# A flow-matching step on one core, its instruction order made with the builder's other machine model

## The chip, the cores and the metric

The kernel runs on one core of a Trainium2 chip. The metric is the device time of one execution in microseconds, as the median of several; less is better. All engines of the core work in parallel on streams of their own: PE (matmuls, and PEld for its weight loads), DVE (VectorE), ACT (ScalarE), POOL (GpSimd) and SP (SyncE, which here issues loads). Each engine takes its instructions strictly in the order of its stream and waits, by semaphores, for what an instruction needs from other engines.

## The reference

One inference step of a two-layer backbone of width 1024, with 512 latent tokens (a grid of 8 rows by 64 columns), 128 prompt tokens and 256 cached prompt keys. Layer 0 mixes tokens by attention with 16 heads: a latent query sees a window of the grid, with a learned bias, and the cached keys, in one softmax; prompt tokens attend among themselves. Layer 1 mixes them by a bidirectional linear recurrent unit (LRU). Each mixer and each feed-forward network (FFN) is wrapped the same way:

```
def _modulate(x, g, shift, scale):
    return _rms_norm(x, g) * (1 + scale[:, None, :]) + shift[:, None, :]
...
def _swiglu(x, w_gu, w_down):
    gate, up = jnp.split(x @ w_gu, 2, axis=-1)
    return (jax.nn.silu(gate) * up) @ w_down
```

The shift, scale and gate vectors come from a conditioning vector times a large matrix (the modulation, six vectors per layer). Each sublayer's output times its gate is added to x. A last RMS norm ends the step, and new keys, values and final LRU states are returned.

## The kernel before, in words

Activations lie transposed, features on the 128 partitions in eight blocks, the 640 tokens along the free dimension. Every product of two float32 matrices is made of three: both operands are split into a high part (a cast by ACT: weights at L180, activations at L1325 and others) and a low part (raw minus high, by DVE: L182 for weights, L1327 for activations), and PE computes high by high (L227), high by low (L228) and low by high (L229), accumulated in PSUM. A weight comes in 512 KB pieces by SP's queue into `raw`, of which there are three, as there are of `whi` and `wlo`. The products go to `mm` tiles (three PSUM buffers), each half of the tokens (320 columns) 24 matmuls long.

The stages, with the times of the profiled execution: start, with norm and first projections (0 to 55 us); attention (55 to 322); its output projection (322 to 370); FFN of layer 0 (370 to 830); LRU (845 to 1005); the LRU's output projection (1005 to 1070); FFN of layer 1 (1070 to 1500); the end.

*Attention.* `attend` goes through eight pairs of heads. A pair is four blocks of 128 queries for each of two heads: eight calls' worth of the body of `softmax`. In that body PE makes the scores `sp` (L831, L832; two buffers), DVE adds the bias and takes the row maximum (a custom instruction, L837), ACT takes the exponential with its row sum (L840), DVE the reciprocal (L842), ACT or DVE scales (L844 for the one head, L846 for the other), PE transposes four times (L849, `tp`, two buffers) and ACT copies (L851). There are three tiles `S` in turn. `softmax_prompt` does the prompt's block of a pair, with scale L878 and transposes L879. The products with the values are L932 (`op`, one buffer), copied by DVE (L939, L941). Beside this run the projections of the next pair: queries and keys (`qk`), low parts at L807, casts at L806, and values (`vq`, L242 to L244, copied at L817). The modulation vectors are put in too: `fill` advances a generator (`mod_cols`) that loads 512 KB of the matrix into `mraw` (two buffers, issued by POOL, L252) and makes two products with row sums on DVE (L256), ten L256 in each of pairs 1 to 5. Each of these is pinned to come behind a certain L837 (`issue_after`).

*LRU.* For each of eight feature blocks: two projections (`lru_xr`, copied by L1263, and `lru_gate`, copied by L1335 with a gelu by L1337 and L1339), a convolution (L1271 on ACT, three L1273 on DVE), four gate products on PE (L1283, each two matmuls into `gp`, two buffers), each with a tanh on ACT (L1284), then exponentials and tanh (L1295, L1296), a square root (L1297), products on DVE (L1285, L1291, L1298, L1299), scans (L1308), sums (L1315, L1316), the product with the gelu (L1320) and the split (L1325, L1327). ACT must load a table of functions (ACT_TABLE_LOAD) when the next function isn't in the loaded one.

*Norm statistics.* Squares on ACT and DVE (L534, L536), column sums by PE with ones (L550, L553), the root on small tiles (L555), a diagonal (L559) and its product that spreads it (L567).

*What sets the order.* The program is written as Python that calls the engines one instruction after another inside a `TileContext`. On leaving that context the builder orders the instructions anew: it runs a model of the machine over them, and each engine's stream is the order in which the model lets its instructions go, held to the data dependencies, the buffers' turns and the pins. Semaphores and ACT's table loads are put in after that. The builder has two such models; an option of the context says which one is run.

## Time and profile before

| what | value |
|---|---|
| median of 2 runs | 1520.13 us (1519.02 to 1521.24) |
| the profiled execution | 1519.85 us, its span 1518.1 us |
| granted PE clock, mean | 0.997 |
| PE, DVE, ACT, POOL busy | 98%, 70%, 46%, 17% of the span |
| DVE busy, 100 to 200 us and 400 to 500 us | 91.6% and 92.5% |

Busy times are unions over a window, so an engine that is at 98% in all can be empty for a few microseconds at several places. Two things help in reading the rows. Back-to-back instructions of an engine overlap, so the distance of two starts, not the printed length, is what one costs. And the waits are listed by the instruction that waited and the instruction that ended the wait. A row of the table by windows has the window, then for PE, PEld, DVE, ACT and POOL the busy us with the count of instructions, the granted PE clock, the share of DMA time and GB/s. A row of a timeline has start, length, engine, line and operation, its tiles (output <- inputs), and in brackets an idle time before it with what ended it.

### The profile page before, as it was taken

The numbers are of one execution on the slowest core, as the hardware profiler recorded it, in microseconds if no ns is written. First come the engines' busy times: TensorE is split into PE (matmuls) and PEld (weight loads), VectorE is DVE, ScalarE is ACT, GpSimd is POOL, SyncE is SP. The second block draws the span as 40 slices with busy tenths as digits, with TensorE's granted clock in tenths as the row PEclk, the third lists the DMA queues.
The fourth block names the chain that finished last, engine by engine and source line by source line (L and its number), as shares of the span: only waits on it lengthen the run. The fifth ranks groups of instructions, "written<-read, shape, count | busy, mean of one in ns | idle before, by whom it ended". The sixth has DMA issues, their size and how long they took to land. (4 is left out here: it accounts for less than half of the span.)

```text
span 1518.1 us, 26165 instructions
## 1 busy us (share of the span) xinstructions
PE 1489.2 (98%) x10397; PEld 1441.2 (95%) x10397; DVE 1062.8 (70%) x2005; ACT 698.3 (46%) x1268; POOL 261.3 (17%) x276
## 2 busy tenths in 40 slices
PE   8999999999999999999999999999999999999997
PEld 5999999899999999999999987799999999999997
DVE  5778998679999997434443769885875665565555
ACT  4576766654332123312321478864634352424243
POOL 0112232100111110000000014230332323232211
PEclk9999999999999999999999999999999999999999
DMA  9555665446556664222222543325242231313211
GB/s 377 172 143 159 188 187 171 118 141 193 180 183 195 207 202 125 62 84 84 65 73 83 158 130 101 115 95 184 74 149 84 70 112 56 111 57 99 69 57 70
DMA packets 72331, 196.66 MB, mean 130 GB/s; under 512 B 8048, under 2 KB 24592, under 8 KB 72080
## 3 DMA queue, kind: packets, MB, share of 16 engines
q1 hardware_dynamic: 57392, 142.32, 29.5%
q0 software_dynamic: 14240, 51.98, 11.2%
q8 instruction: 82, 1.34, 0.4%
q10 hardware_dynamic: 576, 0.68, 0.1%
q14 instruction: 41, 0.34, 0.1%
HBM read 179.48 MB, written 8.92 MB: 124 GB/s over the span
## 5 line engine op out<-in xcount | busy, mean ns | idle before, releaser
L227 PE MATMUL mm<-big,whi 128*128 128x320 f32 (+3 forms) x1233 | 383.6, 313 | 3.2 <-ACT big L1325 2.0
L228 PE MATMUL mm<-big,whi 128*128 128x320 f32 (+3 forms) x1233 | 383.6, 312 | 2.0 <-DVE big L1327 1.8
L229 PE MATMUL mm<-big,wlo 128*128 128x320 f32 (+3 forms) x1233 | 383.5, 312 | 0.0
L227 PEld LDWEIGHTS mm<-big,whi 128*128 128x128 f32 x1233 | 232.7, 189 | 5.8 <-ACT big L1325 2.7
L228 PEld LDWEIGHTS mm<-big,whi 128*128 128x128 f32 x1233 | 233.2, 189 | 4.2 <-DVE big L1327 2.4
L229 PEld LDWEIGHTS mm<-big,wlo 128*128 128x128 f32 x1233 | 232.8, 189 | 1.1
L256 DVE SCALAR_TENSOR_TENSOR mprod<-mraw,csb 128x1024 f32<-128x1024 f32 x160 | 195.1, 1220 | 9.9 <-DMA mraw<-in_wm 9.2
L597 DVE SCALAR_TENSOR_TENSOR x<-mm,G,x 128x320 f32<-128x320 f32 (+2 forms) x192 | 77.8, 435 | 82.0 <-PE mm L229 81.8
L180 ACT CAST whi<-raw 128x1024 fp32r<-128x1024 f32 (+1 forms) x71 | 73.9, 1041 | 113.5 <-PE mm L228 65.2
L182 DVE TENSOR_TENSOR wlo<-raw,whi 128x1024 fp32r<-128x1024 f32 (+1 forms) x87 | 105.5, 1213 | 27.4 <-ACT whi L180 15.6
L227 PE MATMUL mm<-big,whx 128*128 128x320 f32 (+3 forms) x348 | 108.3, 311 | 0.0
L229 PE MATMUL mm<-big,wlx 128*128 128x320 f32 (+3 forms) x348 | 108.0, 310 | 0.0
L228 PE MATMUL mm<-big,whx 128*128 128x320 f32 (+3 forms) x348 | 107.8, 310 | 0.0
L252 POOL DMA_DIRECT2D mraw<-in_wm x80 | 43.0, 537 | 355.8 <-DVE mprod L256 271.5
L227 PE MATMUL mx<-big,whi 128*128 128x320 f32 (+3 forms) x287 | 89.2, 311 | 0.0
L229 PE MATMUL mx<-big,wlo 128*128 128x320 f32 (+3 forms) x287 | 88.8, 310 | 0.0
L228 PE MATMUL mx<-big,whi 128*128 128x320 f32 (+3 forms) x287 | 88.6, 309 | 0.0
L180 ACT CAST whx<-raw 128x1024 fp32r<-128x1024 f32 (+1 forms) x40 | 41.1, 1029 | 87.1 <-PE mm L228 47.9
L227 PE MATMUL mx<-big,whx 128*128 128x320 f32 (+3 forms) x260 | 80.6, 310 | 0.0
L229 PE MATMUL mx<-big,wlx 128*128 128x320 f32 (+3 forms) x260 | 80.5, 310 | 0.0
L228 PE MATMUL mx<-big,whx 128*128 128x320 f32 (+3 forms) x260 | 80.3, 309 | 0.0
L1325 ACT CAST whi<-raw 128x1024 fp32r<-128x1024 f32 (+1 forms) x41 | 41.3, 1008 | 70.8 <-PE mm L228 44.4
(351 smaller groups left out, 3725.7 us busy)
## 6 DMA issues: line engine op xcount, KB each, us to landing
raw<-in_gu SPq DMA_DIRECT2D x88, 512.0 KB, 3.5
mraw<-in_wm POOLq DMA_DIRECT2D x80, 512.0 KB, 4.0
raw<-in_dn SPq DMA_DIRECT2D x24, 512.0 KB, 3.6
sw<-in_wm SPq DMA_DIRECT2D x16, 512.0 KB, 10.1
raw<-in_wqk SPq DMA_DIRECT2D x16, 512.0 KB, 5.0
raw<-in_wi SPq DMA_DIRECT2D x16, 512.0 KB, 3.5
whi<-in_wi POOLq DMA_DIRECT2D x16, 512.0 KB, 3.9
raw<-in_dn SPq DMA_DIRECT2D x16, 448.0 KB, 3.3
```

What stands on the lines that cost most here:

```text
L180: nc.scalar.copy(hi, raw)
L182: nc.vector.tensor_tensor(lo, raw, hi.bitcast(F32), ALU.subtract)
L227: nc.tensor.matmul(ps, hi[:, k], xhi[:, k, s], start=(k == 0), stop=False)
L228: nc.tensor.matmul(ps, hi[:, k], xlo[:, k, s], start=False, stop=False)
L229: self.done = nc.tensor.matmul(ps, lo[:, k], xhi[:, k, s], start=False, stop=(k == last)).ins
L252: nc.gpsimd.dma_start(w, self.i["wm"][l * 6 + j - 2, f])
L256: nc.vector.scalar_tensor_tensor(prod, w, 1.0, self.csb[:, s], ALU.mult, ALU.mult, accum_out=out[:, s, f:f + 1])
L597: self.nc.vector.scalar_tensor_tensor(xs, ps[:, a - t0:b - t0], G[:, s, f:f + 1], xs, ALU.mult, ALU.add)
L1325: self.nc.scalar.copy(hi, v)
```

## The change

One argument of the context: the builder's other model makes the order.

```diff
--- before.py
+++ after.py
@@ -1493,7 +1493,7 @@
     arrays = _lay(inputs)
     ins = {k: nc.dram_tensor(f"in_{k}", v.shape, F32, kind="ExternalInput").ap() for k, v in arrays.items()}
     outs = {k: nc.dram_tensor(f"out_{k}", s, F32, kind="ExternalOutput").ap() for k, s in OUTS.items()}
-    with tile.TileContext(nc, schedule_with_timeline_sim=True) as tc:
+    with tile.TileContext(nc, schedule_with_timeline_sim=False) as tc:
         build(nc, tc, ins, outs)
     r = _run(nc, [{f"in_{k}": v for k, v in arrays.items()}], core_ids=[0]).results[0]
     return _outs({k: r[f"out_{k}"] for k in OUTS})
```

The two programs hold the same instructions (9869 on PE, 1845 on DVE, 1167 on ACT, 279 on POOL, 378 on SP), apart from semaphore instructions and from ACT's table loads, which go from 25 to 29. What changes is the order in each stream. In the attention and in the FFN of layer 1 PE's instructions move most (up to some 25 us against the start times of before); in the FFN of layer 0 they hardly move. Three places follow on which the prediction speaks.

*PE at the end of pair 2 of the attention* (counted from 0). `tp_1804` is the prompt's tile of pair 2 (L879), `sp_2034` and `sp_2035` are the first scores of pair 3, `mm_2342` is a projection for pair 4, `mm_1930` one for pair 3. Before:

```order
L831 MATMUL sp_2034<-KS_1960,QS_1959 128x512
L832 MATMUL sp_2034<-KZ_80_576,QS_1959 128x512
L831 MATMUL sp_2035<-KS_1960,QS_1959 128x512
L832 MATMUL sp_2035<-KZ_80_576,QS_1959 128x512
L227 MATMUL mm_2342<-big_85,whi_2338 128x320
L228 MATMUL mm_2342<-big_86,whi_2338 128x320
```

and, one matmul later,

```order
L227 MATMUL mm_2342<-big_85,whi_2338 128x320
L228 MATMUL mm_2342<-big_86,whi_2338 128x320
L879 MATMUL tp_1804<-ident_63,S_1790 128x128
L229 MATMUL mm_2342<-big_85,wlo_2339 128x320
L879 MATMUL tp_1804<-ident_63,S_1790 128x128
L227 MATMUL mm_2369<-big_85,whi_2338 128x320
```

After, at the prompt's transposes:

```order
L229 MATMUL mm_1930<-big_85,wlo_1900 128x320
L227 MATMUL mm_1930<-big_85,whi_1899 128x320
L228 MATMUL mm_1930<-big_86,whi_1899 128x320
L879 MATMUL tp_1804<-ident_63,S_1790 128x128
L229 MATMUL mm_1930<-big_85,wlo_1900 128x320
L879 MATMUL tp_1804<-ident_63,S_1790 128x128
```

and, 89 instructions behind these, at the first scores of pair 3:

```order
L227 MATMUL mm_2342<-big_85,whi_2338 128x320
L831 MATMUL sp_2034<-KS_1960,QS_1959 128x512
L832 MATMUL sp_2034<-KZ_80_576,QS_1959 128x512
L228 MATMUL mm_2342<-big_86,whi_2338 128x320
L229 MATMUL mm_2342<-big_85,wlo_2339 128x320
```

Before, the next pair's first scores and the projection for pair 4 stand ahead of the prompt's transposes. After, the transposes come earlier, in the middle of the projection for pair 3, with the rest of that projection and the next ones behind them, and then the next pair's scores.

*DVE in the middle of pair 2.* `wlo_2339` is the low part of the weight of `mm_2342`, the lines L771 and L807 belong to the queries of pair 3. Before:

```order
L256 SCALAR_TENSOR_TENSOR mprod_1675,G_187_1092<-mraw_1671,csb_81 128x1024
L182 TENSOR_TENSOR wlo_2339<-raw_2336,whi_2338 128x1024
L771 TENSOR_SCALAR r_1833<-mm_1868 128x8x8
L842 RECIPROCAL rc_1707<-sm_1705 128x1
L837 ISA S_1717,nm_1718<-sp_1697,bt_1586 128x512
L837 ISA nm_1718 128x1
L256 SCALAR_TENSOR_TENSOR mprod_1734,G_187_1092<-mraw_1732,csb_81 128x1024
L846 TENSOR_SCALAR S_1702<-S_1702,rc_1707 128x512
L807 TENSOR_TENSOR r_1833<-r_1833,QS_1959 64x640 x2
L256 SCALAR_TENSOR_TENSOR mprod_1736,G_187_1092<-mraw_1732,csb_81 128x1024
L837 ISA S_1744,nm_1745<-sp_1738,bt_1579 128x512
```

After:

```order
L256 SCALAR_TENSOR_TENSOR mprod_1675,G_187_1092<-mraw_1671,csb_81 128x1024
L842 RECIPROCAL rc_1707<-sm_1705 128x1
L837 ISA S_1717,nm_1718<-sp_1697,bt_1586 128x512
L837 ISA nm_1718 128x1
L846 TENSOR_SCALAR S_1702<-S_1702,rc_1707 128x512
L256 SCALAR_TENSOR_TENSOR mprod_1734,G_187_1092<-mraw_1732,csb_81 128x1024
L842 RECIPROCAL rc_1722<-sm_1720 128x1
L837 ISA S_1744,nm_1745<-sp_1738,bt_1579 128x512
L837 ISA nm_1745 128x1
L939 COPY big_568<-op_1677 128x128 x2
L256 SCALAR_TENSOR_TENSOR mprod_1736,G_187_1092<-mraw_1732,csb_81 128x1024
```

The weight's low part and the queries' work have left this stretch; L771 comes just ahead of the pair's L878, L182 and L807 behind it. The softmaxes' instructions and the modulation's L256 stand next to each other.

*ACT at the end of the LRU.* `gp_10622` is the last gate product, `lt_10441` and `lt_10608` are tiles of the last two blocks, `whi_10883` is the high part of the first weight of the LRU's output projection. Before, from the tanh of the last gate product on:

```order
L1284 ACTIVATE lt_10609<-gp_10622,l_hb_2016 128x643
L1296 ACTIVATE lt_10441<-lt_10441,l_sp_386_2012 128x643
L1335 COPY gl_10645<-mm_10652 128x384
L1296 ACTIVATE lt_10441<-lt_10441,l_sp_386_2012 128x643
L1296 ACTIVATE lt_10608<-lt_10608,l_sp_386_2012 128x643 x2
L180 CAST whi_10883<-raw_10881 128x1024
L1337 ACT_TABLE_LOAD
L1337 ACTIVATE gl_10645<-mm_10678 128x256
L1339 ACTIVATE gl_10645<-gl_10645 128x384
L1297 ACT_TABLE_LOAD
L1297 ACTIVATE lt_10441<-lt_10441 128x1286
```

After, from the fifth instruction behind that tanh on:

```order
L1337 ACT_TABLE_LOAD
L1337 ACTIVATE gl_10645<-mm_10678 128x256
L1297 ACT_TABLE_LOAD
L1297 ACTIVATE lt_10441<-lt_10441 128x1286
L1339 ACT_TABLE_LOAD
L1339 ACTIVATE gl_10645<-gl_10645 128x384
L1295 ACT_TABLE_LOAD
L1295 ACTIVATE lt_10708<-lt_10608,l_sm_387_2014 128x643
L1325 CAST big_9509<-lt_10520 128x640
```

and a few rows on:

```order
L1337 ACT_TABLE_LOAD
L1337 ACTIVATE gl_10726<-mm_10759 128x256
L1297 ACT_TABLE_LOAD
L1297 ACTIVATE lt_10608<-lt_10608 128x1286
L1339 ACT_TABLE_LOAD
L1339 ACTIVATE gl_10726<-gl_10726 128x384
L1335 COPY gl_10798<-mm_10805 128x384
L1337 ACTIVATE gl_10798<-mm_10831 128x256
L1339 ACTIVATE gl_10798<-gl_10798 128x384
L180 CAST whi_10883<-raw_10881 128x1024
```

The weight's cast stood ahead of the first of these table loads; now it stands behind the last gelu, with seven loads between that tanh and it, where before there were none. On DVE the low part of the same weight (L182) moves with it, from ahead of the L1298 of the last two blocks to behind the last scan.

## The prediction

> **What bounds the kernel now.** First the page's head and the list of what PE waits for.
>
> ```profile
> span 1518.1 us, 26165 instructions
> PE 1489.2 (98%) x10397; PEld 1441.2 (95%) x10397; DVE 1062.8 (70%) x2005; ACT 698.3 (46%) x1268; POOL 261.3 (17%) x276
> ```
>
> ```profile
> PE gp L1283 <- ACT lt L1284: 2.3, 2, 1.9
> PE mm L227 <- ACT big L1325: 2.0, 3, 0.8
> ```
>
> PE is busy for 1489.2 of 1518.1 us. The two rows are the largest of its waits: 28.9 us of idle time lie in pieces of 2 us or less. So PE is the limit, and an order can give back at most those 28.9 us; it can take away as much as it likes, by letting PE arrive somewhere before its operands. Next the table by stage, for the price of a matmul and for where the idle time lies.
>
> ```profile
> 500.00:600.00 100.00, 100.00 (x680) 100.00 (x679) 88.28 (x158) 23.88 (x41) 10.56 (x20) 1.00 0.57 184
> 900.00:1000.00 100.00, 94.00 (x558) 82.27 (x557) 86.90 (x101) 87.40 (x116) 33.98 (x20) 1.00 0.34 104
> ```
>
> A matmul of 320 columns costs 100/680 = 0.147 us where PE runs without a gap. Only the stretch of the LRU (900 to 1000) has PE clearly below full, with ACT and DVE both at 87%. The attention, which the change reorders most, goes through eight pairs of heads, counted here from 0; pair 2 reads
>
> ```profile
> 133.70:166.30 32.60, 32.60 (x263) 31.14 (x262) 29.96 (x80) 21.54 (x49) 8.07 (x11) 1.00 0.70 197
> ```
>
> PE without a gap, DVE at 92%: DVE is the second bound there, and the new order has to be weighed against DVE.
>
> **The change, term by term.** No instruction is added or removed except table loads of ACT (25 before, 29 after). Everything else is order, so each term is: when does PE reach a matmul, and when is its operand ready.
>
> *Attention, pairs 1 to 5.* In the order of before, the projections of the next pair stand among all of a pair's eight softmaxes. In the new order the softmaxes stand close together and 89 to 96 PE instructions, most of them projections, come behind the prompt's transposes (L879). DVE's work per pair up to L878, which L879 waits for, must then fit beside less PE work. What DVE instructions cost back to back is read from the distance of starts, since they overlap:
>
> ```profile
> 137.92 0.48 DVE L846 TENSOR_SCALAR S<-S,rc 128x512 f32<-128x512 f32 x1
> 138.32 0.69 DVE L837 CUSTOM_DVE_ANT_1 S<-sp,bt 128x512 f32<-128x512 f32 x1
> 138.93 0.09 DVE L837 DVE_READ_ACCUMULATOR2_ANT nm<- 128x1 f32 x1
> ...
> 144.23 0.16 DVE L842 RECIPROCAL rc<-sm 128x1 f32<-128x1 f32 x1
> 144.31 1.21 DVE L256 SCALAR_TENSOR_TENSOR mprod<-mraw,csb 128x1024 f32<-128x1024 f32 x1
> 145.44 0.08 DVE L256 DVE_READ_ACCUMULATOR mprod<-mraw,csb 128x1 f32 x1
> ```
>
> So L846 costs 0.40, L837 0.61, L842 0.08 and L256 1.13 us. In pair 3 there stand from its first L837 to its second L878 8 L837, 10 L256, 8 L842, 4 L846 and 11 small ones: 4.9 + 11.3 + 0.6 + 1.6 + 2.0 = 20.4 us (the small ones lie between 0.08 and 0.40; I take 0.18). Pairs 1 and 5 have the same; pairs 2 and 4 also hold one L182, as large as L256: 21.5. PE's work up to L879 is counted in the same way.
>
> ```profile
> 171.06 0.39 PE L831 MATMUL sp<-KS,QS 128*128 128x512 f32 x1
> 171.29 0.40 PE L832 MATMUL sp<-KZ,QS 128*128 128x512 f32 x1
> ...
> 176.18 0.66 PE L849 MATMUL tp<-ident,S 128*128 128x128 f32 x4
> 176.59 0.48 PE L831 MATMUL sp<-KS,QS 128*128 128x512 f32 x1
> ```
>
> A score matmul costs 0.23, a transpose 0.41/4 = 0.10 us. In pair 2 there are, behind the first score, 14 score matmuls, 78 of a projection and 52 small ones: 3.3 + 11.5 + 5.4 = 20.2; in the other pairs 20 to 20.6. I walked pair 3 by hand through the new order with these prices and 0.1 us for each passing between engines: DVE stands still for 1.2 us (it waits for a free S buffer twice), and L879 starts 1.2 us after PE reached it. With L182 in the way it is 2.3. Three pairs at 1.2 and two at 2.3 give **+8.2**; behind L879 PE has 11 to 13 us of work and DVE 7 to 12, so that is not given back. Lower bound 0 (the S waits fall away). The upper bound comes from the vectors' weights: the ten L256 of a pair now take five buffers in 20 us with two to fill in turn.
>
> ```profile
> mraw<-in_wm POOLq DMA_DIRECT2D x80, 512.0 KB, 4.0
> ```
>
> Issue to landing is 4.0 us, a buffer comes round every 8, and the two L256 that hold it take about 3: a slack of 1 us per buffer, so up to 3 us more per pair, +15, if landing slows by that much.
>
> *Pair 6, second half.* Before, two gaps for wo's operands stand in this row, and then the clock falls:
>
> ```profile
> 290.00:293.60 3.60, 1.49 (x10) 1.18 (x10) 3.51 (x7) 3.59 (x6) 1.55 (x4) 1.00 1.00 261
> 293.60:297.10 3.50, 3.50 (x13) 3.50 (x14) 3.50 (x6) 3.26 (x8) 1.57 (x2) 0.51 0.81 188
> ```
>
> After, six score products stand in one block at the end of that pair with two score buffers, and L849 waits for an ACT scale that stands behind two casts (L806): my walk gives waits of 0.4, 0.8, 2.0, 1.3 and some small ones, 4.9 us, for the 2.1 that go: **+2.5** (bounds 0 and 5). Pairs 0 and 7 walk through with 0.5 each: **+1**.
>
> *LRU.* The four gate matmuls L1283 of a block now come close together and earlier, the block's projections after them in one piece. In my walk of two blocks PE waits 0.9 us, some 3 over the stretch 900 to 1000, where before it stands idle for 6.0. **-3** (bounds -6 and +4).
>
> *End of the LRU.* Here two rows of order decide. The first weight cast of the output projection (L180 whi) stood before the last two square roots; now it stands behind the last gelu, with seven table loads ahead of it instead of none.
>
> ```profile
> 992.84 1.73 ACT L1296 ACTIVATE lt<-lt,l_sp 128x643 f32<-128x643 f32 x2
> 994.47 1.04 ACT L180 CAST whi<-raw 128x1024 fp32r<-128x1024 f32 x1
> 995.53 1.28 ACT L1337 ACT_TABLE_LOAD   x1
> 996.82 0.38 ACT L1337 ACTIVATE gl<-mm 128x256 f32<-128x256 f32 x1
> 997.10 0.52 ACT L1339 ACTIVATE gl<-gl 128x384 f32<-128x384 f32 x1
> 997.63 1.28 ACT L1297 ACT_TABLE_LOAD   x1
> 998.93 2.45 ACT L1297 ACTIVATE lt<-lt 128x1286 f32<-128x1286 f32 x2
> ```
>
> Distance of starts: 0.82 for L1296 (L1295 is as large), 0.96 to 1.06 for L180, 1.29 for a table load, 0.28 for L1337, 0.42 to 0.53 for L1339, 1.22 for L1297. From the last gate tanh to the end of that cast ACT now has 4 L1296, 3 L1295, 2 L1297, 3 each of L1335, L1337 and L1339, one L1325, the tanh and L180. L1335, L1325 and the tanh, between 320 and 643 elements, I take at 0.4, 0.6 and 0.7 (estimates between the 0.28 of L1337's 256 and the 0.82 of L1296's 643). That makes 13.9 us, and the loads 9.0: 22.9. PE has in this time 134 matmuls of the last projections, 19.5 us, and ACT comes to that tanh some 1.6 us late: PE waits 5.0. The low half of the weight (L182) is worse, on DVE behind the last scan.
>
> ```profile
> 1000.24 2.91 DVE L1298 SCALAR_TENSOR_TENSOR lt<-lt,lt 128x1286 f32<-128x1286 f32 x2 [1.77 <-ACT lt L1297]
> 1003.07 1.49 DVE L1299 TENSOR_TENSOR lt<-lt,lt 128x1286 f32<-128x1286 f32 x1
> 1004.48 1.22 DVE L182 TENSOR_TENSOR wlo<-raw,whi 128x1024 fp32r<-128x1024 f32 x1
> ...
> 1007.76 1.28 DVE L1308 TENSOR_TENSOR_SCAN lt<-lt,cols,lt 128x512 f32<-128x512 f32 x1
> 1008.95 0.40 DVE L1308 TENSOR_TENSOR_SCAN lt<-lt,lt 128x128 f32<-128x128 f32 x1
> 1009.27 1.26 DVE L1308 TENSOR_TENSOR_SCAN lt<-lt,cols,lt 128x512 f32<-128x512 f32 x1
> ...
> 1014.86 1.31 DVE L1315 TENSOR_TENSOR lt<-lt 128x64 f32<-128x64 f32 x2
> 1016.05 0.32 DVE L1316 TENSOR_TENSOR lt<-lt 128x128 f32<-128x128 f32 x1
> ```
>
> From the end of the second L1297 on: L1298 1.4, L1299 1.4, L1320 0.7 (half as wide as L1299), scans 2 x 1.5, the sums L1315 and L1316 with one split 2.2, L182 1.1: 9.8 us. PE's cover was used up 0.9 us before that L1297 ends, and 1.5 us of first products can be done meanwhile: it loses 9.2 in all. Before it lost 0.8 a little later (part of the L1325 row above): **+8.4** (bounds +3, if DVE runs ahead, and +11).
>
> [...]
>
> *The rest.* Output projection of the attention, the two FFNs and the norm statistics: a split or a statistic that comes earlier, with 0.5 to 1 us less cover, at some six places: **+4** (bounds 0 and 8). In the FFNs PE otherwise keeps its blocks whole, with three buffers in front of evictions that DVE does in time.
>
> *Clock.* Row 293.60 shows a granted clock of 0.51 for 3.5 us after 2.1 idle in 3.6. A single gap of 1.87 us did not do that (the stretch 900 to 1000 shows 1.00):
>
> ```profile
> 915.48 1.35 PE L1283 MATMUL gp<-xc,gw 128*128 128x512 f32 x4 [1.87 <-ACT lt L1284]
> ```
>
> Pair 6 has its dip before and after. The end of the LRU gets one: half of 3.5 us, **+1.7** (bounds 0 and +5).
>
> *Passing between engines.* L837 lasts 0.69 where the next starts after 0.61, so a consumer on another engine sees 0.08 more than my walks took; some 35 such passings at places where PE waits: **+3**.
>
> Sum: 8.2 + 2.5 + 1 - 3 + 8.4 + 4 + 1.7 + 3 = 25.8. The profiled execution took 1519.85 us, 1.75 more than its span and 0.28 below the median of the two runs: 1545.7 by its own time, and **1546 us** against the median, 1.7% more.
>
> **Rivals.** *The bursts go over (1568).* If the vectors' weights land late in the bursts, DVE stands still at L256: +15 by the bound above, waits of about 4 us at L879. A window of 3.5 us mostly idle then halves the clock for the next one, as in row 293.60, at 1.7 us for four of the five pairs, near 7: 1546 + 22 = 1568. For it: DVE is at 92% already. Against it: the slack is positive on paper. It decides from a landing of 5 us.
>
> [...]
>
> *Most of it is absorbed (1529).* DVE runs ahead in the tails, so the bursts cost 0.5 each, the LRU gains 3 and only its end and some waits elsewhere (6 and 3.4) remain: 1520.1 + 2.5 - 3 + 6 + 3.4 = 1529. For it: DVE's tails in pairs 1, 3 and 5 are 4 us shorter than PE's. Against it: the next pair's scores stand at the end of PE's tail, so DVE has nothing to run ahead with.
>
> *The other side (1514).* Mechanism: gate matmuls side by side take away all 6.0 us of the LRU's idle time, its end is covered because ACT comes early to its last chain, and the other waits find DVE ahead: 1520.1 - 6 = 1514. It decides at the first wo product of layer 1: whether its high cast is there within 19.5 us of the last gate product. Against it: seven loads counted above.
>
> That the change moves nothing is excluded, since the orders differ.
>
> **Numbers.** Chances: forecast 0.40 (its own range 1536 to 1556), bursts over 0.33, absorbed 0.20, other side 0.07. 2% above the median, about what a measurement of this kernel can tell from no change, is 1550.5. Over it lie nearly all of the first rival and a third of the forecast: 0.33 x 0.97 + 0.40 x 0.35 = 0.46. Faster by over 2% would need more idle time than there is: 0.02. The rest, 0.52, is the same. Range 1522 to 1578: from the absorbed case less half of the LRU's bound up to the first rival with one more dip; outside lie the other side and the rest of the first rival.
>
> **What would show it.** In the new profile: PE waits "tp L879 <- DVE S L878" of 1 to 2.5 us, five or six times; "mm L227 <- ACT whi L180" and "mm L229 <- DVE wlo L182" together near 9 us just after the last LRU projection, with the clock below 1 behind them; gp L1283 waits of 4 us or less in all; 29 table loads. The prediction is wrong if L879 shows no wait (DVE's burst was not the bound), if the LRU loop loses more than before, or if FFN stretches fall below 99% of PE.

## The result, and the profile after

The changed kernel takes 1622.5 us (median of 2 runs, 1616.9 to 1628.2) against 1520.1: a ratio of 1.068, 95% interval 1.0645 to 1.0715. It is slower by 102 us, where 26 were forecast and 58 was the upper end of the range. The profiled execution's head:

```profile
span 1615.1 us, 26169 instructions
PE 1521.9 (94%) x10397; PEld 1458.1 (90%) x10397; DVE 1062.7 (66%) x2005; ACT 705.5 (44%) x1272; POOL 256.2 (16%) x276
```

The span grew by 97.0 us (1518.1 to 1615.1). PE is idle for 93.2 us of it where it was idle for 28.9, so 64.3 us are new waits (in both kernels some 7 to 8 us of the idle time lie in one piece behind PE's last matmul, so not all of the 28.9 are short waits, as the prediction reads them). The other 32.7 are PE's busy time (1489.2 to 1521.9) with the same 10397 instructions. Up to some 23 of them are the clock: its granted mean fell from 0.997 to 0.983, which is 0.017 of 1615.1 us less 0.003 of 1518.1. The rest is probably stops too short to show as idle time, since a matmul's row is 0.31 us long where the next one starts 0.147 us later. What PE waits for, the seven largest (total us, times, longest):

```profile
PE mc L1097 <- DVE g L1108: 31.3, 13, 3.7
PE mm L227 <- DVE x L597: 6.9, 6, 2.3
PE mm L227 <- ACT whi L180: 5.7, 1, 5.7
PE tp L849 <- ACT S L844: 3.7, 8, 2.0
PE gp L1283 <- DVE xc L1273: 3.5, 4, 1.4
PE tp L879 <- DVE S L878: 3.2, 3, 1.7
PE mm L229 <- DVE wlo L182: 2.7, 1, 2.7
```

Five of the seven rows are named in the prediction or lie in its stages, each with a few microseconds. The first two do not occur in it: 31.3 us in thirteen waits for `mc`, and 6.9 us in six waits for an `mm` tile that DVE's L597 (a product added to x) has to empty. The table by stage says where they are. The stages are cut at the same places of the program in both kernels; the counts of matmuls differ, since the order moves some over the cuts, so idle times compare better than lengths. They are attention pairs 1 to 5; pair 6; the LRU's gate products; the LRU's end; the pairs of the FFN of layer 1. The columns are the window, its length, and busy us (instructions) of PE, PEld, DVE, ACT and POOL, then the granted clock. Before:

```profile
101.90:265.10 163.20, 163.20 (x1374) 155.95 (x1373) 149.29 (x384) 110.17 (x237) 41.56 (x53) 1.00 0.59 174
265.10:300.10 35.00, 32.67 (x244) 30.17 (x243) 24.89 (x58) 25.35 (x52) 6.55 (x10) 0.95 0.45 128
873.30:986.30 113.00, 107.19 (x611) 90.58 (x611) 92.38 (x105) 92.04 (x125) 31.18 (x22) 1.00 0.37 115
986.30:1053.40 67.10, 65.64 (x448) 64.61 (x447) 46.54 (x66) 34.23 (x47) 13.40 (x7) 1.00 0.43 148
1112.30:1482.10 369.80, 369.53 (x2505) 368.79 (x2505) 218.43 (x347) 141.24 (x227) 99.29 (x72) 1.00 0.27 82
```

After:

```profile
104.00:288.40 184.40, 173.92 (x1399) 161.11 (x1399) 155.46 (x390) 113.13 (x243) 38.91 (x53) 0.99 0.55 160
288.40:323.00 34.60, 30.41 (x198) 27.39 (x197) 20.80 (x48) 23.25 (x47) 5.83 (x10) 0.90 0.44 125
898.40:1016.90 118.50, 111.28 (x633) 93.78 (x634) 97.51 (x111) 94.20 (x128) 35.42 (x23) 1.00 0.40 116
1016.90:1090.00 73.10, 63.76 (x408) 62.29 (x407) 41.55 (x57) 37.49 (x49) 15.28 (x7) 0.91 0.38 131
1155.80:1573.40 417.60, 379.24 (x2466) 373.37 (x2465) 212.52 (x347) 142.17 (x227) 96.78 (x72) 0.97 0.24 73
```

Length less PE's busy time is PE's idle time. It goes from 0.0 to 10.5 in pairs 1 to 5, from 2.3 to 4.2 in pair 6, from 5.8 to 7.2 at the LRU's gates, from 1.5 to 9.3 at its end, and from 0.3 to 38.4 in the FFN of layer 1. That last stage alone grew by 47.8 us: half of the loss, in a place that the prediction had only within its +4 for the rest. All thirteen waits for `mc` lie there, and five of the six for L597 (5.2 us).

What is done there has to be known for the rest. The FFN of layer 1 makes each pair of a gate and an up block in seven half-sized products (lines 1092 to 1144) from sums of quarters of the weights. For a pair SP loads the gate weights (L1059) and the up weights (L1069) into `raw`; ACT and DVE split the gate's first half into `whi` and `wlo`; GpSimd makes four sums from both (L1075, into two `sum` tiles), which are split into `whx` and `wlx`; the up weights' second half is split into `wuh` and `wul`. All these splits are the function `split`, cast L1325 on ACT and subtract L1327 on DVE. PE's products go to PSUM tiles `mm` and `mx` (three each) and `mc`, of which there is one. A pair's S1 product opens `mc`, its last product S4 closes it, and DVE's L1108 evicts it. So the next pair's S1 cannot start before that eviction, and between S4 and that S1 the new order leaves PE one product (12 matmuls, 1.8 us), except where a whole down projection lies there. In the order of before there are two products at eight of the 18 places and only 5 to 7 matmuls, some 1 us or less, at five. PE waited 0.3 us in all in that stage, because DVE stood ready for the eviction, as this row of before shows:

```profile
DVE g L1108 <- PE mc L1099: 11.9, 16, 1.6
```

Sixteen times DVE waited for S4. After, that row has one wait of 0.2 us: DVE comes late instead. One turn, in the timeline of the changed kernel (start, length, engine, line, tiles, and in brackets the idle time before with what ended it; the rows are put together from the engines' own timelines):

```profile
1278.18 0.33 SPq L1059 DMA_DIRECT2D raw<-in_gu  x1
...
1281.74 1.04 ACT L1325 CAST whi<-raw 128x1024 fp32r<-128x1024 f32 x1 [4.66 <-DMA raw<-in_gu]
...
1282.81 1.23 DVE L1327 TENSOR_TENSOR wlo<-raw,whi 128x1024 fp32r<-128x1024 f32 x1 [4.55 <-ACT whi L1325]
...
1284.36 0.48 DVE L1108 TENSOR_TENSOR g<-mc,snap 128x320 f32<-128x320 f32 x1
1284.76 0.68 DVE L1327 TENSOR_TENSOR wul<-raw,wuh 128x512 fp32r<-128x512 f32 x1
1284.90 0.42 PE L1097 MATMUL mc<-big,whx 128*128 128x320 f32 x1 [3.65 <-DVE g L1108]
...
1285.52 0.33 SPq L1069 DMA_DIRECT2D raw<-in_gu  x1
...
1289.27 2.27 POOL L1075 TENSOR_TENSOR sum<-raw 128x512 f32<-128x512 f32 x1 [11.11 <-ACT whx L1325]
...
1295.45 0.39 SPq L189 DMA_DIRECT2D raw<-in_dn  x1
```

The rows of SP are loads being issued. The load of the next gate weights goes out at 1278.18, as soon as GpSimd's sums have released a buffer of `raw` (the last starts at 1276.86 and takes 1.30 us). ACT's next instruction in order is its cast, and ACT stands still for 4.66 us until it lands. DVE's next instruction is the subtract behind that cast, and DVE stands still for 4.55. Behind these two stand the eviction (1284.36, half a microsecond of work on data that PE had finished at 1279.49) and the small split `wul` (1284.76). PE waits 3.65 us for the eviction. And `wul` releases the up weights' buffer, so the next up load goes out only at 1285.52, the four sums that need it start at 1289.27 and end at 1295.43, and the load that these hold up leaves at 1295.45. From load to load it is 17.3 us; seven products are 12.3. The largest wait for L597 has the same form, three `mm` buffers or not: DVE stands for 3.05 us before a subtract `wlx` (1170.51) whose cast is late, L597 behind it starts at 1171.76, and PE has waited 2.32 us. The bracket at 1289.27 names a cast of ACT that had just ended; the sum reads the up load, issued 3.75 us earlier, and the page's median of these loads from issue to landing (last number) fits:

```profile
raw<-in_gu SPq DMA_DIRECT2D x88, 512.0 KB, 3.5
```

### The profile page after: what moved, and what is told of

The parts are those of the page before. It is cut to its first block, busy times and chain, and to the rows that moved or that the text cites. A ratio compares the mean times of both kernels' runs of the same rounds, so it can differ in the third digit from the quotient of the medians.

```text
span 1615.1 us, 26169 instructions
## 1 busy us (share of the span) xinstructions
PE 1521.9 (94%) x10397; PEld 1458.1 (90%) x10397; DVE 1062.7 (66%) x2005; ACT 705.5 (44%) x1272; POOL 256.2 (16%) x276
## 5 line engine op out<-in xcount | busy, mean ns | idle before, releaser
L256 DVE SCALAR_TENSOR_TENSOR mprod<-mraw,csb 128x1024 f32<-128x1024 f32 x160 | 197.9, 1237 | 23.8 <-DMA mraw<-in_wm 23.1
L182 DVE TENSOR_TENSOR wlo<-raw,whi 128x1024 fp32r<-128x1024 f32 (+1 forms) x87 | 105.2, 1210 | 38.0 <-ACT whi L180 33.0
L597 DVE SCALAR_TENSOR_TENSOR x<-mm,G,x 128x320 f32<-128x320 f32 (+2 forms) x192 | 77.3, 436 | 78.8 <-PE mm L229 78.7
L1325 ACT CAST whi<-raw 128x1024 fp32r<-128x1024 f32 (+1 forms) x41 | 41.2, 1006 | 106.6 <-PE mm L228 36.8
L1327 DVE TENSOR_TENSOR wlo<-raw,whi 128x1024 fp32r<-128x1024 f32 (+1 forms) x41 | 51.7, 1261 | 54.7 <-ACT whi L1325 54.5
L227 PE MATMUL mx<-big,whx 128*128 128x320 f32 (+3 forms) x260 | 80.6, 310 | 0.0
L1097 PE MATMUL mc<-big,whx 128*128 128x320 f32 x152 | 51.1, 336 | 31.3 <-DVE g L1108 31.3
```

The lines of the kernel that those rows point to most:

```text
L182: nc.vector.tensor_tensor(lo, raw, hi.bitcast(F32), ALU.subtract)
L227: nc.tensor.matmul(ps, hi[:, k], xhi[:, k, s], start=(k == 0), stop=False)
L256: nc.vector.scalar_tensor_tensor(prod, w, 1.0, self.csb[:, s], ALU.mult, ALU.mult, accum_out=out[:, s, f:f + 1])
L597: self.nc.vector.scalar_tensor_tensor(xs, ps[:, a - t0:b - t0], G[:, s, f:f + 1], xs, ALU.mult, ALU.add)
L1097: nc.tensor.matmul(ps, hi[:, k], xh[:, k], start=start and k == 0, stop=False, skip_group_check=not start)
L1325: self.nc.scalar.copy(hi, v)
```

## The experiments

All are the changed kernel with one edit, unless said otherwise; each time stands beside the kernel before on the same chip (1518.1 to 1519.2 us).

**The splits behind the eviction** (`pin_splits`). `tots` holds, for each pair, DVE's eviction and ACT's activation behind it.

```diff
 def gate_weights(self, l, f):
...
-        self.split(hi, lo, raw)
+        self.split(hi, lo, raw, self.tots.get(f - 3, (None, None)))
...
-    def project_part(self, w, hi, lo, gk, also=None):
+    def project_part(self, w, hi, lo, gk, also=None, after=(None, None)):
...
-            for f, u in zip((k, k + KH), self.two(w[k::KH], False)):
+            for f, u in zip((k, k + KH), self.two(w[k::KH], False, after)):
...
-                self.project_part(w, self.hhi, self.hlo, (l, 5), rest if f0 == PLAIN else None)
+                self.project_part(w, self.hhi, self.hlo, (l, 5), rest if f0 == PLAIN else None, self.tots.get(f0 - 2, (None, None)))
```

> The changed kernel with one thing put back: in the second FFN the casts and subtracts that split the next weights (lines 1325 and 1327, from the gate weights and from the down projection's pieces) are queued on ScalarE and VectorE behind the eviction of the running pair of products; TensorE's order is untouched. Theory A (a split of later weights stands at the head of both queues and waits for its load, and the 0.5 us eviction of the single mc buffer stands behind it): the 3 us waits of line 1097 for line 1108 go, the stretch from the first to the last product of that FFN falls from 418 us to 375-385 us, the kernel from 1622 to 1578-1592 us. Rival B (the down projection's products now stand in one piece instead of between the pairs, so nothing covers the eviction of the one mc buffer): TensorE's order is the same, so the waits stay at 1 to 3 us each and the kernel stays above 1610 us.

Measured: 1581.9 us, ratio 1.0419 (1.0389 to 1.0448), 40 us less. The waits for `mc` and the stage:

```profile
PE mc L1097 <- DVE g L1108: 3.0, 1, 3.0
```

```profile
1160.10:1538.50 378.40, 368.36 (x2466) 365.13 (x2465) 223.94 (x347) 143.49 (x227) 100.90 (x72) 0.99 0.27 81
```

One wait is left of thirteen (the last projection's weights, which this edit did not pin), and the stage is down from 417.6 to 378.4 us with PE's order unchanged. Rival B, that products no longer lie between the pairs, falls: one product is cover enough when DVE is in time. The pin moves more than the eviction, though: in its trace `wul` (1286.33) and the eviction (1287.59) both run ahead of the split (1290.94). Which of them counts is asked below. The five waits for L597 stay (5.7 us); this edit does not pin the splits of the sums, behind which L597 stood.

**Four buffers for the raw weights** (`raw4`).

```diff
-        raw = self.t([P, KT, P], F32, "raw", 3)
+        raw = self.t([P, KT, P], F32, "raw", 4)
```

This line stands for six: every place that makes a `raw` tile is changed so.

> The changed kernel with four instead of three buffers for the raw weights, everywhere. Rival C (the loads come late because the third buffer is freed late, by the sums on GpSimd): loads are issued one buffer earlier, the 3 us waits in the second FFN go, 1578-1592 us. Theory A (the builder's model takes a load as landed sooner than it is, and places the split by that): the splits move up in the queues with the buffers, as the order of this kernel shows them do, and still wait for their loads at the queues' heads; the waits shrink little, 1605-1620 us.

Measured: 1583.3 us, ratio 1.0425 (1.0394 to 1.0456). Theory A's number is missed and rival C's is met. The stage, and what ACT waits for there; first four buffers, then the changed kernel:

```profile
1156.40:1535.40 379.00, 366.97 (x2465) 363.58 (x2465) 221.29 (x347) 144.44 (x227) 100.08 (x72) 1.00 0.26 79
```

```profile
ACT whi L1325 <- DMA raw<-in_dn: 13.7, 8, 2.8
```

```profile
ACT whi L1325 <- DMA raw<-in_dn: 27.0, 10, 4.6
ACT whi L1325 <- DMA raw<-in_gu: 24.8, 8, 4.7
```

The waits of the casts for gate loads (24.8 us, eight times) don't appear any more, and those for down loads are halved. PE's waits for `mc` are down to 3.6 us in four. The splits moved up in the queues, as theory A said, but the loads moved up further. So the fault needs both: a split at the head of the queues, and a load that is not there.

**Which of the two things behind the split costs** (`pin_wul`): the small split goes ahead of the late one, the eviction stays behind it. `lasts` holds the pair's `wul` and `wuh`.

```diff
-        self.split(hi, lo, raw)
+        self.split(hi, lo, raw, self.lasts.get(f - 2, (None, None)))
```

The down projection's pieces get the same pin.

> The changed kernel with one swap in the second FFN: the small split of the last weights (wuh and wul, 0.61 us on ScalarE and 0.68 us on VectorE) is queued ahead of the split of the next gate or down weights, not behind it; the eviction of mc (line 1108) stays behind that split as in the changed kernel. Theory L (a loop sets the pace: the late split holds back wul, wul holds the raw buffer of the up weights, so their next load, the sums on GpSimd and the next gate load all start late; 17.3 us a turn against 12.3 us of products): the loop is cut, loads come in time, the waits for mc go though the eviction's place is unchanged, 375-390 us from the first to the last product and 1578-1595 us in all. Theory A as first put (what costs is that the eviction itself stands behind the split): the waits for mc stay at 2 to 3.5 us, 1605-1622 us.

Measured: 1604.6 us, ratio 1.0558 (1.0527 to 1.0589). The waits for `mc` and the stage:

```profile
PE mc L1097 <- DVE g L1108: 20.0, 13, 2.7
```

```profile
1164.00:1563.30 399.30, 373.81 (x2465) 367.95 (x2464) 222.62 (x347) 143.76 (x227) 96.54 (x72) 0.98 0.25 76
```

The stage takes 399.3 us: 18.3 of the 39.2 us that the pin gave. The waits neither go, as theory L had it, nor stay: thirteen are left, with 20.0 us where there were 31.3. The kernel's time lies between both theories' ranges. One turn of it:

```profile
1280.94 0.33 SPq L1059 DMA_DIRECT2D raw<-in_gu  x1
...
1282.53 0.69 DVE L1327 TENSOR_TENSOR wul<-raw,wuh 128x512 fp32r<-128x512 f32 x1
1283.25 0.33 SPq L1069 DMA_DIRECT2D raw<-in_gu  x1
...
1284.39 1.05 ACT L1325 CAST whi<-raw 128x1024 fp32r<-128x1024 f32 x1 [1.89 <-DMA raw<-in_gu]
...
1287.01 0.48 DVE L1108 TENSOR_TENSOR g<-mc,snap 128x320 f32<-128x320 f32 x1
1287.41 1.21 DVE L1327 TENSOR_TENSOR wlx<-sum,whx 128x1024 fp32r<-128x1024 f32 x1
...
1288.76 1.41 POOL L1075 TENSOR_TENSOR sum<-raw 128x512 f32<-128x512 f32 x1 [7.84 <-DVE wlx L1327]
...
1295.38 0.38 SPq L189 DMA_DIRECT2D raw<-in_dn  x1
```

`wul` now runs at 1282.53 and the up load leaves at 1283.25, 2.3 us behind the gate load instead of 7.3. But the cast still waits for its load (1284.39). Behind it stand the eviction (1287.01) and `wlx` (1287.41), which releases the `sum` tile; the next sums start at 1288.76, as it ends, and the next load leaves at 1295.38. The loop is 14.4 us where it was 17.3, and still longer than the products. So neither theory holds alone: everything behind the late split is held back, the eviction that PE waits for and the releases from which the next load starts. The two edits that cure it put the split behind both, or have its load there.

**Is the half clock a second price?** (`keep_warm`) PE works on something useless while it waits.

```diff
...
         q["c"] = c = self.ps("mc")[:, 0:HT]
+        self.keep(self.ps("at"), 10 if j > 1 else 0)
```

> The changed kernel with ten extra matrix products of the identity (line 210, 0.275 us records, about 3 us together), whose result nothing reads, on TensorE ahead of the S1 product of each third and fourth pair of the second FFN, where it waits 2.0 to 3.7 us for the mc buffer. The waits stay as they are. Theory (each such wait is paid twice, since the 12 or 13 products behind it run at 0.27 us instead of 0.15): the products behind keep 0.15 us and 1.2 to 1.7 us are saved at nine places, 10 to 15 us in all, 1607-1612 us. Rival (the half clock there has another cause than TensorE's rest): no gain, and up to 5 us lost where the extra products outlast the wait.

Measured: 1621.3 us, ratio 1.0664 (1.0627 to 1.07): no gain. A wait and the stretch behind it, in the changed kernel and then here, with the whole stage as the last row:

```profile
1281.25:1284.90 3.65, 0.00 (x1) 0.01 (x1) 2.09 (x4) 2.87 (x4) 0.00 (x0) 1.00 0.00 1
1284.90:1288.30 3.40, 3.40 (x13) 3.40 (x14) 2.57 (x4) 1.47 (x4) 0.00 (x0) 0.54 0.53 147
```

```profile
1290.30:1291.90 1.60, 0.00 (x1) 0.01 (x1) 1.60 (x4) 1.31 (x3) 0.00 (x0) 1.00 0.00 0
1291.90:1295.40 3.50, 3.50 (x24) 3.50 (x25) 3.02 (x5) 2.30 (x4) 0.00 (x0) 1.00 0.53 140
1163.40:1579.90 416.50, 391.44 (x2646) 385.84 (x2645) 210.16 (x347) 141.71 (x227) 94.08 (x72) 0.99 0.24 73
```

In the changed kernel 13 matmuls run in 3.40 us behind 3.65 us of rest, at a granted clock of 0.54. Here 24 run in 3.5 us, at 1.00. So the theory's first half holds here: with a shorter rest the half clock is gone, and over the stage the granted clock is 0.99 instead of 0.97. Its second half falls: the stage is 416.5 us against 417.6. Of PE's 391.44 us the useless products are 21.5, so the others take 369.9 where they took 379.2. PE gets these 9 us back and loses them again: useless products and waits for `mc` (16.8 us) are 38.3 together where the waits were 31.3. PE reaches the next wait earlier and waits longer there. That fits a loop of loads, splits and sums that sets the pace and hardly runs over PE; half clock cost nothing in this stretch.

**The end of the LRU** (`lru_dma`).

```diff
-        if self.ptags == ["at"]:
+        if self.ptags == ["at"] or dma:
             nc.gpsimd.dma_start(hi, src)
...
-        us = [self.unit(w[f], "m") for f in range(3)]
+        us = [self.unit(w[f], "m", None, True) for f in range(3)]
```

> The changed kernel with the first three weights of the recurrence's out projection cast by a casting DMA from GpSimd's queue instead of by ScalarE (line 180), as the recurrence's own weights are. Theory (the cast stands on ScalarE behind the last block's activations and their table loads, and TensorE waits 5.7 us for it and 2.7 us for the subtract behind it): both waits go, 8 to 12 us less, 1610-1614 us. Rival (TensorE would wait there for the last blocks of the recurrence itself, line 1327's y): another wait takes the place, at most 3 us less, 1619-1623 us.

Measured: 1612.3 us, ratio 1.0614 (1.0588 to 1.064), 10 us less. The stage after:

```profile
1020.10:1083.10 63.00, 60.45 (x408) 58.90 (x407) 41.73 (x57) 35.30 (x46) 11.60 (x10) 1.00 0.54 177
```

It was 73.1 us with a clock of 0.91. PE's idle time falls from 9.3 to 2.6 and some 3 of the 10 us are busy time of the same 408 matmuls, at a clock of 1.00. The cast behind the last block's activations was the cause.

**The modulation products** (`late_mods`).

```diff
-        self.fill((0 < p < 6) + (b == 3 and 0 < p < 5))
+        self.fill(0 < p < 6 and b < 3)
...
-            nc.vector.tensor_scalar(s[:, a], s[:, a], sm[:, a:a + 1], None, ALU.mult)
+            self.anchor = nc.vector.tensor_scalar(s[:, a], s[:, a], sm[:, a:a + 1], None, ALU.mult).ins
...
         nc.scalar.copy(pt, tp[:, 0:256])
+        self.fill((0 < p < 6) + (0 < p < 5))
```

> The changed kernel with the modulation products (line 256) of each pair's fourth block traced after the prompt block and queued on VectorE behind its normalisation (line 878), same products in all. Theory (in pairs 1 to 5 four of them, 1.22 us each, run between line 868 and line 878, and TensorE's transposes of line 879 wait for it): the waits of line 879 on line 878 (3.2 us in three places) and what stands behind them go, and with the time at half clock after each of them 5 to 10 us in all, 1612-1617 us. Rival (VectorE is the bound of these pairs, 95% busy or more, so the wait only moves to the rope's lines 766 to 807 or to line 846): within 2 us of the changed kernel.

Measured: 1616.9 us, ratio 1.0646 (1.0617 to 1.0674). Pairs 1 to 5, and PE's two largest waits in them:

```profile
104.30:282.40 178.10, 172.02 (x1400) 159.88 (x1399) 153.96 (x390) 111.71 (x243) 37.24 (x53) 1.00 0.56 165
```

```profile
PE sp L831 <- DMA KS<-KS: 3.7, 2, 2.1
PE tp L879 <- DVE S L878: 1.0, 3, 0.4
```

L879 waits 1.0 instead of 3.2 us, PE's idle time is 6.1 instead of 10.5 (a new wait, for DMA-moved keys, is most of it), and the stretch is 178.1 us instead of 184.4. The kernel's time alone does not show the gain, since its interval overlaps that of the changed kernel (1.0645 to 1.0715). The stretch does: in the five runs that edit only other stages and keep three raw buffers it takes 185.2 to 188.2 us, in the two with all repairs below 177.8 and 179.9. The theory holds for these 6 us. Half clock, which it adds behind each of these waits, is not there in the changed kernel: behind the two longest, 1.66 us (it ends at 129.11) and 1.25 us (at 202.55), the clock is 1.00 in the next 3.40 us.

**The splits of the head outputs in pair 6** (`late_split`).

```diff
-                if p == 6:
+                if p == 7:
                     ohi = self.big()
...
-                        self.split(ohi[:, k], olo[:, k], O[:, k], self.parted)
+                        self.split(ohi[:, k], olo[:, k], O[:, k], (self.anchor, None))
```

> The changed kernel with the splits of seven heads' outputs (line 1327, 0.82 us each) traced in the last pair instead of in pair 6, behind its softmax. Theory (in pair 6 they stand ahead of the softmax's steps on VectorE, and TensorE waits 4.2 us there): pair 6 waits 1 us or less and the kernel gains 3 to 7 us, 1615-1620 us. Rival (the out projection starts right behind and now waits for these splits instead): the wait after the end of attention grows from 1.8 us by as much, within 2 us of the changed kernel.

Measured: 1626.7 us, ratio 1.0718 (1.0686 to 1.0751): no gain. PE's waits in pair 6:

```profile
PE sp L866 <- DVE nm L837: 2.4, 1, 2.4
PE tp L849 <- ACT S L844: 1.8, 1, 1.8
```

They add up to what they were. The theory falls, and the rival's sign is missing too: in the attention's output projection (345.5 to 407.8) PE is idle for 0.4 us. The wait that the prediction walked for this place (L849 for ACT's scale, 2.0 us) was the right one and does not run over these splits.

**The repairs together** (`combo`: `pin_splits` with the last projection's weights pinned too, `lru_dma`, `late_mods`), with four raw buffers besides (`combo_raw4`), and, on the kernel before, the buffers (`before_raw4`) and the pins (`before_pins`) alone.

> The changed kernel with the three repairs together, and the pin put on the last projection's weights too. If the three causes are separate (the queue heads in the second FFN -40 us, the cast at the end of the recurrence -10, the modulation products ahead of the prompt softmax -6, the last 3.0 us wait for mc with its half clock about -4), their sum from 1622 us is 1560-1568 us. If they share their cover (a wait that is taken away in one place comes back in the next), it stays above 1575 us.

> The same with four buffers for the raw weights. If the pins and the fourth buffer are two cures of one fault (either the split doesn't stand ahead of the eviction, or its load has landed), the buffer adds nothing: within 6 us of the three repairs alone. If late loads do harm of their own (first weights of a stage, the projection's pieces), 10 us or more are gained.

> The kernel before, with the order of the first model, and four buffers for the raw weights. If the fault is the pairing of this load time with the second model's order, the first has nothing to cure: within 0.5% of before. If the third buffer is too few in itself, 8 us or more are gained.

> The kernel before, with the order of the first model, and the pins of the second FFN. Its splits do not wait for a load ahead of an eviction (TensorE waits 0.3 us in all in that stretch), so the pins have nothing to take away: within 0.5% of before, and slower rather than faster, since they change the order in which the products are laid between the pairs.

Measured: 1561.8 us, ratio 1.0282 (1.026 to 1.0304); 1556.7, 1.0252 (1.0231 to 1.0274); 1523.1, 1.0036 (1.0022 to 1.0049); 1520.4, 1.0013 (1.0 to 1.0025). The three causes add up as forecast, to 61 of the 102 us. The fourth buffer adds at most little to the pins (the intervals overlap), and neither cure helps the kernel before: the fault belongs to the new order. The head of the repaired kernel:

```profile
PE 1503.3 (97%) x10397; PEld 1442.7 (93%) x10397; DVE 1072.9 (69%) x2005; ACT 703.6 (45%) x1269; POOL 252.4 (16%) x279
```

Of its span of 1555.7 us PE is idle for 52.4, 23.5 more than before, and busy for 14.1 more. Apart from the kernel's first load (2.8 us) and its end, the idle time lies in many waits of 2.5 us or less; the largest row left is the one of L597, 7.3 us in six waits. The busy time is not the clock, which is 0.997 as before. Which rows of order make these 37.6 us was not tried one by one, and their cause stays open. No version found beats the kernel before.

## Why the prediction was wrong, step by step

*The rest: failed.* The prediction put +4 us on the output projection, both FFNs and the statistics, bounds 0 and 8, because "in the FFNs PE otherwise keeps its blocks whole, with three buffers in front of evictions that DVE does in time". In the FFN of layer 1 the stage table has 38.1 us of new waits. The sentence is false in three ways there. The eviction that matters most has one buffer, `mc`. Those with three buffers come late too, L597 five times (5.2 us). And "in time" was true of the order of before (DVE waited for S4 sixteen times) but not of the new one: DVE's load hardly changed, 218 us before and 213 after; what changed is what stands ahead of the eviction in DVE's and ACT's queues. The attention and the LRU were walked through the new order; this stage, where PE's order moved as far, was not. The bounds came from places counted at 0.5 to 1 us each, so they could not hold a loop that repeats with every pair. `pin_splits` puts 40 us of the result on this step. Outside that stage the term was about right: from pair 7 to the LRU's first blocks (323.0 to 898.4, before 300.1 to 873.3) PE's idle time went from 3.0 to 7.5 us.

*Attention, pairs 1 to 5: mechanism right, the number partly luck.* Forecast +8.2, all of it at L879; measured 10.5 us of waits, of which L879 has 3.2, in three places and not five or six. The others are at lines that the walk does not name: L768 2.2, L817 1.8, L844 1.7, L771 1.5. The modulation products are behind some of these as well: ahead of that L771 (163.73) DVE does an L256 of 1.21 us (162.52), and `late_mods`, which moves such products, takes away the rows of L768, L771 and L817. PE's busy time grew by 10.7 us besides; 25 more matmuls inside the cuts are some 4 of them, the rest was not worked out. The walk's 0.1 us for each passing between engines was the author's estimate and has no row; where DVE's accumulator read of 138.93 in the kernel before ends (139.02), ACT's next instruction starts at 139.05, 0.03 us later.

*Pair 6: right.* Forecast +2.5, measured +1.9, with L849 behind ACT's scale at 2.0 us, as in the walk.

*LRU: wrong sign, small.* Forecast -3, measured +1.4. The walk gave 3 us of waits and the stage has 7.2; half of them are the row "gp L1283 <- DVE xc L1273", the convolution's result, which the prediction does not name.

*End of the LRU: right.* Forecast 9.2 us of waits in the two rows named; measured 5.7 + 2.7 = 8.4, and `lru_dma` takes them away.

*Clock: mis-sized.* One dip, +1.7, was put in the sum; by the mean granted clock up to 23 us more were lost than before. Not all of that is a price: in the FFN of layer 1 a matmul took 379.24/2466 = 0.154 us instead of 369.53/2505 = 0.148, some 15 us over the stage, and `keep_warm` took 9 of these back for no gain. At the LRU's end some 3 of the 10 us regained are clock. Behind the rest of 3.65 us from 1281.25 the clock was 0.54 for 3.40 us, the rows that stand with `keep_warm`; behind other rests, one of 3.56 us among them, it stayed at 1.00 (last section).

*Pairs 0 and 7 (+1), passing between engines (+3): open.* No run isolates them.

*The rivals.* "The bursts go over" named another stage; its 1568 us were nearer by the wrong cause. Its condition, a landing of 5 us, did not come: in pairs 1 to 5 the vectors' weights landed after 3.9 us (median of 23), and DVE waited for them 2.5 us in all. That a window mostly idle halves the clock for the next, which it takes from one row, did not hold throughout (last section). The last sentence of the prediction did name the sign of the failure, an FFN below 99% of PE: it is at 379.2 of 417.6, 91%.

## What to carry to other kernels

When only an order changes, ask at each tile with a single buffer what stands ahead of its eviction in the evicting engine's queue, and whether that waits for a load: DVE, busy for 212.5 of the 417.6 us (51%), was late here for an eviction of 0.48 us. Where a split of prefetched data (a cast and a subtract of weights loaded ahead of use) stands there, look for the loop from its releases back to its own load, and compare the loop's turn with the compute of a turn; a prefetched operand's conversion belongs behind the work that releases buffers, or needs a buffer more (here 1581.9 and 1583.3 us against 1622.5). A wait's half clock is to be added only where PE sets the pace: in `keep_warm` the granted clock rose from 0.97 to 0.99, and the stage went from 417.6 to 416.5 us.

## What the hardware showed besides

In these runs the length of a rest does not decide by itself whether the clock is halved behind it. Two stretches of the changed kernel, the first behind a rest of 2.32 us (from 1170.26), the second behind one of 3.56 us (from 1549.68):

```profile
1172.50:1175.90 3.40, 3.33 (x12) 3.36 (x13) 2.65 (x5) 0.00 (x0) 0.00 (x0) 0.50 0.20 23
1553.25:1556.70 3.45, 3.45 (x23) 3.45 (x24) 2.97 (x5) 2.29 (x4) 0.00 (x0) 1.00 0.76 189
```

Behind the shorter rest 12 matmuls took 3.33 us at a clock of 0.50, behind the longer one the clock stayed at 1.00. So half clock followed the shorter rest and not the longer one. Rests of 2.26 us (from 1239.48) and 2.24 us (from 1389.91) left it at 1.00 too, for the 3.45 us that followed. What decides besides the length is not shown by these runs.

In the turn shown, GpSimd's first sum took 2.27 us where its next took 1.30. A subtract of DVE (`wlx`, 1289.16) ran beside it. Of the 76 sums L1075 of the changed kernel, 50 had no subtract L1327 beside them and took 1.28 to 1.31 us; all ten over 1.4 us had one, as had 16 of the others. That the two share something was not tried.
